# Both FF pairs run alone with block-product down projections, and the sample's attention moves beside the prompt's projections

## The chip, the cores and the metric

One core of a Trainium2 chip runs the whole kernel. The metric is device time in microseconds (us) of one execution, lower is better; of several executions the median is taken. Beside it stands one execution recorded by the hardware profiler, from which all rows below come. Engines: PE (TensorE, with its weight loads as PEld), DVE (VectorE), ACT (ScalarE), POOL (GpSimd), SP (SyncE, which issues nearly all DMAs).

## The reference, cut to what matters

Two independent sequences go through the same two layers: a prompt of 1024 rows and a sample of 512 rows, each 1024 wide. All is float32.

```
def run_trunk(x):                      # x_prompt (1, 1024, 1024), x_sample (1, 512, 1024)
    x = x + fourier_mixer(x, ...)                       # layer 0: FFT over rows and groups, then @ w
    x = x + swiglu_ffn(x, ...)
    x = x + attention_mixer(x, ...)                     # layer 1
    x = x + swiglu_ffn(x, ...)

def attention_mixer(x, g, w_qkv, q_gain, k_gain, w_o, cos, sin):
    q, k, v = split(rms_norm(x, g) @ w_qkv)             # 8 query heads, 2 key/value heads of 128
    q = apply_rope(rms_norm(q, q_gain), cos, sin)       # norm per head; k in the same way
    p = softmax(q @ k.T * 128 ** -0.5)                  # each query head with its group's k
    return (p @ v) @ w_o

def swiglu_ffn(x, g, w_gate, w_up, w_down):             # D_FF = 2816
    h = rms_norm(x, g)
    return (silu(h @ w_gate) * (h @ w_up)) @ w_down
```

## The kernel before, in words

**Tiles.** Activations lie transposed: 128 channels on the partitions, 512 rows along the free dimension. So the sample is one block (block 0) of 8 chunks of 128x512, the prompt two (blocks 1 and 2). D_FF is NF = 22 chunks of 128. Each float32 operand is split into a rounded high part and a remainder (`split`: ACT casts, POOL or DVE subtracts), and each product is three matmuls (`mm3`: high x high, high x low, low x high), the lines L255, L256 and L257 of the profile. Weights are loaded by SP (L289) and split by ACT and POOL (L293, L294).

**Stages.** Mixing of the sample; FF of the sample's layer 0 (`ffn(0, 0)`) beside mixing of the prompt (`aux_0`); "pair 0", the FF of both prompt blocks together in layer 0 (`ffn_pair`), beside the sample's layer-1 chain (`aux_1`: `qkv(0)`, `attend((0,), ...)`, `out_projection(0)`, `prepare(0, 1)`, the norm ahead of its FF); the sample's last FF (`ffn(1, 0)`) beside the prompt's layer 1 up to its FF (`aux_2`: `qkv(2)`, `qkv(1)`, `attend((1, 2), ...)`, two output projections, `moving`); then "pair 1" alone, to the end.

**A pair.** `moving` makes seven operands (`OPERANDS`: B11, B21, T2, T1, B22, T3, N4) from the normed two blocks and stores them in DRAM (`mov`). Gate and up are computed as seven block products instead of eight: for each couple of FF chunks f0, f0+1, `step` runs `times` for each operand, eight products each, with the weights' sums made by POOL (`operands`, `stationary`). The operands come through a ring of eight buffers, unless `places` gives one a place of its own, where it stays after its first load. `times` calls `some` after each product, which adds a credit, and with a whole credit takes one item from the list `pend`: products of the down projection, which run one couple of chunks behind.

**Two ways down.** With `wide` False (pair 0), `down` adds for each block and each of 8 output chunks the products of the two FF chunks, and DVE adds their sum to the accumulator at L1019. With `wide` True (pair 1), `product` runs seven block products (`CHAINS`) of four output chunks each, on operands that `operands_down` and `values_of` make, and DVE adds each at L1107. `wide` also pins some POOL operations in program order (`keep`), takes another order of turns, and loads a21 and a22 earlier.

**Attention.** `qkv` makes twelve heads for one block: eight q, two k, two v. Each is a projection (`project`, 24 matmuls), a square for the head's norm, rotary products on ACT and DVE, four small matmuls that sum the squares (L1341), and a store to DRAM (`dqk`, `dv`). For k, `rstd_cols` and `in_rows` follow (four diagonal tiles by ACT, a matmul with ones each: L322, L323). `attend` takes for each head and each 128 query rows three steps: `scores` (products, a maximum on DVE at L1398, its scaling at L1399, the exponential on ACT at L1402, reciprocal and scaling at L1403 and L1404), `turned` (transposes at L1416, and their splits), and for each two of them `values`. The steps of neighbours overlap: scores of the next come before the transposes of the last.

**The order.** `weave(main, main_cost, aux, aux_cost, lead)` draws from two generators in turn: each yields an estimate of its work in us, and the one that is behind, as a share of its cost, goes next; `lead` steps of the main one go first. Main draws from the buffer rings ending in F, aux from those in X (`cur`; `BUFS` has their depths: w weights, raw loads, t temporaries, g and c banks of PSUM). The framework then orders each engine's instructions by its own model of their times, in which program order is the priority; a buffer ring that is full makes the next tile wait. While pair 0 runs, the X rings are small (`narrow`, `thin()`). SP's DMAs are in one queue.

Of the kernel before, what the change touches and what calls it, by code (L numbers as in the profile page):

```python
# [17 lines left out]
P = 128  # L18
# [107 lines left out]
def trunk_kernel(ctx: ExitStack, tc: tile.TileContext, t: dict):  # L126
# [18 lines left out]
    for name, kw in (("sbH", {}), ("sbF", {}), ("sbX", {}), ("psF", PS), ("psX", PS)):  # L145
# [46 lines left out]
    narrow = [False]  # L192

    def thin():

        return narrow[0] and cur[0] == "X"

# [6 lines left out]
    def side():  # L204

        return bankg() if cur[0] == "F" else bank() if thin() else bank2()[:, 0]
# [110 lines left out]
    def in_rows(y, temp=None, ps=None):  # L317

        r = bank() if ps is None else ps
        for j in range(4):  # L320
            dg = (temp or tmp)(P)
            act.activation(dg, ident, AF.Copy, scale=y[:, j : j + 1])  # L322
            pe.matmul(r[:, j * P : (j + 1) * P], ones, dg, start=True, stop=True)  # L323
        return r
# [36 lines left out]
    def normed(b, gain, got, ab, held=None):  # L361
# [4 lines left out]
        if thin():  # L366
            r, seen = tl("r", [TB], F32, "ssX"), r
            act.copy(r, seen)
        h = h_tile(ab)
        yield 1.0  # L370
        for dp in range(NC // 2):
            for dc, ps in zip((2 * dp, 2 * dp + 1), (None, None) if thin() else sides()):
# [5 lines left out]
                ps = x if ps is None else ps  # L378
# [553 lines left out]
    def ffn_pair(layer, blocks, ring, places, wide, outs):  # L932
# [37 lines left out]
        keep = pinned if wide else lambda ins: ins  # L970
# [23 lines left out]
        wds, coming = {}, {}  # L994

        def load_down(fc):
            coming[fc] = raw_tile(D)
            sp.dma_start(coming[fc], t["down"][layer, fc])

        def fetch_down(fc):  # L1000
            wds[fc] = w_tile(2, NC, P)
            flat = wds[fc].rearrange("p h c n -> p h (c n)")
            split(flat[:, 0], flat[:, 1], coming.pop(fc), eng=pool)

        def down(b, parts, dc, begins, ends):

            box, acc = [], accs[b][dc]

            def half(k):
                n, fc = parts[k]  # L1010
                m, wd = slots[n], wds[fc]
                open_[n] -= 1
                if k == 0:
                    box.append(bank())
                    if begins:
                        sp.dma_start(acc, xres[b][:, dc, :])
                mm3(box[0], wd[:, 0, dc], wd[:, 1, dc], m[:, 0], m[:, 1], k == 0, k + 1 == len(parts))
                if k + 1 == len(parts):
                    dve.tensor_tensor(acc, box[0], acc, op=ALU.add)  # L1019
                    if ends:  # L1020
                        new_residual(b, dc, acc, None if outs is None else outs[b][:, dc, :], room=spare, later=sums_of(b, dc))

            return [lambda k=k: half(k) for k in range(len(parts))]

        mids = {b: [] for b in blocks}
        two = [tl("mid", [2, TB], F32R, "mid") for _ in range(2)]
        if wide:
            spots = two + [tl("mid", [2, TB], F32R, "m2", raws) for _ in range(4)] + [ring[:, 7]]
            spots = dict(zip(("M11", "T1", "T2", "T3", "M22", "M21", "N4"), spots))
            f11, f12 = (tl("f", [TB], F32, "f2", raws) for _ in range(2))  # L1030
        else:
            slots = [two[0], two[1], tl("mid", [2, TB], F32R, "m2", raws), ring[:, 7]]
        open_ = [0] * 4
        where = {(0, 0): (0, 1), (0, 1): (1, 0), (1, 1): (2, 2), (1, 0): (3, 3)}

        def downs(b, f0):

            parts, mids[b] = mids[b], []
            lists = [down(b, parts, dc, f0 == 0, f0 + 2 == NF) for dc in range(NC)]
            for k in range(len(parts)):  # L1040
                pend.extend([lists[0][k], lists[1][k]])
            for v in lists[2:]:
                pend.extend(v)
# [46 lines left out]
        def product(k, d, f0):  # L1090
# [50 lines left out]
        def before_down(f0):  # L1141

            if not wide:
                downs(blocks[1], f0)
            elif f0 == 0:
                load_acc(blocks[0], 0)
# [22 lines left out]
        turn = [0]  # L1169

        TURNS = (tuple((i, j) for j in range(4) for i in range(2)), ((0, 0), (0, 1), (1, 0), (0, 2), (0, 3), (1, 1), (1, 2), (1, 3)))

        def times(w, name, f0, hook, at):

            turn[0] += 1
            if turn[0] % 2 == 0 and not wide:
                banks = [bankg(), bankg()]
            else:
                g2 = tl("a", [2, TB], F32, "gT", gt)
                banks = [g2[:, 0], g2[:, 1]]  # L1180
            at_hand, xs = name in places and f0 > 0, {}
            for n, (i, j) in enumerate(TURNS[wide]):
# [14 lines left out]
        def hidden(up, s, fc, k):  # L1197
            dve.tensor_tensor(up, up, s, op=ALU.mult)
            n = where[fc % 2, k][fc // 2 % 2]
            assert not open_[n], (fc, k)  # L1200
            open_[n] = NC
            m = slots[n]
            split(m[:, 0], m[:, 1], up)
            mids[blocks[k]].append((n, fc))

# [7 lines left out]
        def operands():  # L1213

            a11, a12 = quarter(0, 0), quarter(0, 1)
            for f0 in range(0, NF, 2):
                yield stationary(a11)
                if not (wide and f0):
                    a21, a22 = quarter(f0 + 1, 0), quarter(f0 + 1, 1)
                s1 = tl("raw", [2, TB], F32, "rT", raws) if wide else raw_tile(2, TB)  # L1220
# [12 lines left out]
                if wide and f0 + 2 < NF:  # L1233
# [14 lines left out]
        for f0 in range(0, NF, 2):  # L1248
            f1 = f0 + 1
            gates = {}  # L1250

            def finish(k, ps, s):

                if wide:
                    values_of(k, ps, gates[k], s)
                else:
                    hidden(ps, s, *((f0, 0), (f0, 1), (f1, 1), (f1, 0))[k])
# [16 lines left out]
            for i, ps in (yield from step("T1", lambda: load_rows_down(f0) if wide else load_down(f0), 0)):  # L1274
                plus(V[i], ps, U[i])
            for i, ps in (yield from step("B22", lambda: prepare_down(f0) if wide else (fetch_down(f0), load_down(f1)), 0)):
# [5 lines left out]
            for i, ps in (yield from step("T3", lambda: next(preps[-1]) if wide else fetch_down(f1), 0)):  # L1282
# [6 lines left out]
            for i, ps in (yield from step("N4", lambda: before_down(f0), 0 if wide else 1)):  # L1289
# [5 lines left out]
            if wide:  # L1295
                pend.extend(lambda k=k, d=d, f0=f0: product(k, d, f0) for k in range(7) for d in range(4))
            else:
                downs(blocks[0], f0)
        while pend:
            pend.pop(0)()  # L1300
        close_pool("gT")
# [3 lines left out]
    def qkv(b, held=None):  # L1305
# [6 lines left out]
        ssq = cols.tile([P, 4, NH], F32, tag="ssq", name=nm("ssq"))  # L1312
        for j in range(NH + 2 * NKV):
# [403 lines left out]
```

## Time and profile before

| | |
|---|---|
| median of 3 executions | 2982.39 us (2978.16 to 2984.53) |
| profiled execution | 2986.82 us, span 2984.9 us from the first to the last instruction |
| granted TensorE clock, mean | 0.987 |
| PE busy | 2881.0 us, 97%, 13788 matmuls |
| DVE, ACT, POOL busy | 1606.1, 1281.3 and 1421.0 us |
| DMA | 559.73 MB, 188 GB/s in the mean |

A group's row reads: line, engine, operation, tiles written <- read, shapes, xcount | busy us, mean ns of one | idle time of the engine just ahead of these, and what ended most of it. A row by stage gives the stretch and its width, then busy us and (xcount) of PE, PEld, DVE, ACT and POOL, the granted clock, the DMA engines' share and GB/s. A row of waits says who waited for whom: us in total, times, longest. A row of one line's instructions gives their shortest, median and longest duration in ns, and the first and last start. Matmuls overlap their neighbours, so the mean duration of one is longer than the spacing of two.

### The profile page before, as it was taken

The numbers are of one execution on the slowest core, as the hardware profiler recorded it, in microseconds if no ns is written. First come the engines' busy times: TensorE is split into PE (matmuls) and PEld (weight loads), VectorE is DVE, ScalarE is ACT, GpSimd is POOL, SyncE is SP. The second block draws the span as 40 slices with busy tenths as digits, with TensorE's granted clock in tenths as the row PEclk, the third lists the DMA queues.
The fourth block names the chain that finished last, engine by engine and source line by source line (L and its number), as shares of the span: only waits on it lengthen the run. The fifth ranks groups of instructions, "written<-read, shape, count | busy, mean of one in ns | idle before, by whom it ended". The sixth has DMA issues, their size and how long they took to land. (4 is left out here: it accounts for less than half of the span.)

```text
span 2984.9 us, 37275 instructions
## 1 busy us (share of the span) xinstructions
PE 2881.0 (97%) x13788; PEld 2378.8 (80%) x13788; DVE 1606.1 (54%) x2822; ACT 1281.3 (43%) x2032; POOL 1421.0 (48%) x833
## 2 busy tenths in 40 slices
PE   7999999999999999999999999999998999999999
PEld 6878877878888787877788778788876778888887
DVE  6665553453436554346434365555426366666666
ACT  5543242333325564223444367777534333333332
POOL 4344365545434445434433311212345666776774
PEclk8999999999999999999999999999999999999999
DMA  7335484887767667776533311211457966556553
GB/s 225 142 120 174 150 302 144 289 271 253 245 234 242 222 225 255 270 257 225 190 112 111 104 53 40 78 40 64 129 185 261 332 233 231 192 184 219 200 173 126
DMA packets 201333, 559.73 MB, mean 188 GB/s; under 512 B 21984, under 2 KB 32224, under 8 KB 200256
## 3 DMA queue, kind: packets, MB, share of 16 engines
q1 hardware_dynamic: 200224, 552.57, 54.4%
q0 software_dynamic: 640, 3.74, 0.4%
q8 instruction: 108, 1.77, 0.2%
q10 hardware_dynamic: 288, 1.05, 0.1%
q14 instruction: 73, 0.60, 0.1%
HBM read 489.12 MB, written 68.16 MB: 187 GB/s over the span
## 5 line engine op out<-in xcount | busy, mean ns | idle before, releaser
L294 POOL TENSOR_TENSOR w<-raw,w 128x1024 fp32r<-128x1024 f32 x200 | 479.2, 2404 | 816.6 <-ACT w L293 793.9
L249 POOL TENSOR_TENSOR w<-raw,w 128x512 fp32r<-128x512 f32 (+1 forms) x420 | 577.2, 1396 | 553.1 <-ACT w L248 549.2
L248 ACT CAST w<-raw 128x512 fp32r<-128x512 f32 (+1 forms) x420 | 261.3, 655 | 455.8 <-PE a L257 127.8
L293 ACT CAST w<-raw 128x1024 fp32r<-128x1024 f32 x200 | 208.7, 1049 | 286.3 <-PE g L257 78.8
L255 PE MATMUL c<-mid,w 128*128 128x512 f32 x748 | 295.1, 395 | 14.6 <-DVE acc L1019 7.0
L257 PE MATMUL c<-mid,w 128*128 128x512 f32 x748 | 292.6, 391 | 2.3 <-POOL w L294 2.3
L256 PE MATMUL c<-mid,w 128*128 128x512 f32 x748 | 292.8, 391 | 2.0 <-DVE mid L249 2.0
L255 PE MATMUL g<-h,w 128*128 128x512 f32 x704 | 281.1, 399 | 9.7 <-ACT w L293 7.7
L257 PE MATMUL g<-h,w 128*128 128x512 f32 x704 | 279.4, 397 | 3.3 <-POOL w L294 3.3
L256 PE MATMUL g<-h,w 128*128 128x512 f32 x704 | 279.2, 397 | 0.0
L255 PE MATMUL a<-ring,w 128*128 128x512 f32 x664 | 262.4, 395 | 5.7 <-DVE ring L249 4.5
L257 PE MATMUL a<-ring,w 128*128 128x512 f32 x664 | 259.4, 391 | 0.0
L256 PE MATMUL a<-ring,w 128*128 128x512 f32 x664 | 259.3, 390 | 0.0
L1019 DVE TENSOR_TENSOR acc<-c,acc 128x512 f32<-128x512 f32 x176 | 120.8, 688 | 148.9 <-PE c L257 143.5
L256 PE MATMUL c<-h,w 128*128 128x512 f32 x480 | 190.1, 396 | 4.2 <-POOL h L249 2.8
L255 PE MATMUL c<-h,w 128*128 128x512 f32 x480 | 190.6, 397 | 2.4 <-ACT h L251 1.7
L257 PE MATMUL c<-h,w 128*128 128x512 f32 x480 | 188.5, 393 | 0.0
L792 DVE TENSOR_TENSOR acc<-c,acc 128x512 f32<-128x512 f32 x176 | 120.5, 687 | 122.1 <-PE c L257 121.2
L255 PEld LDWEIGHTS c<-mid,w 128*128 128x128 f32 x748 | 140.5, 188 | 51.5 <-DVE acc L1019 10.6
L257 PEld LDWEIGHTS c<-mid,w 128*128 128x128 f32 x748 | 140.5, 188 | 32.5 <-POOL w L294 3.6
L256 PEld LDWEIGHTS c<-mid,w 128*128 128x128 f32 x748 | 140.7, 188 | 31.8 <-DVE mid L249 3.6
L255 PEld LDWEIGHTS g<-h,w 128*128 128x128 f32 x704 | 134.1, 191 | 36.9 <-ACT w L293 8.5
(393 smaller groups left out, 6564.7 us busy)
## 6 DMA issues: line engine op xcount, KB each, us to landing
ring<-mov_B SPq DMA_DIRECT2D x248, 512.0 KB, 5.5
ring<-mov_T SPq DMA_DIRECT2D x176, 512.0 KB, 5.1
raw<-in_gate_dram SPq DMA_DIRECT2D x44, 512.0 KB, 3.5
raw<-in_up_dram SPq DMA_DIRECT2D x44, 512.0 KB, 3.6
raw<-in_down_dram SPq DMA_DIRECT2D x88, 256.0 KB, 3.1
raw<-in_gate_dram SPq DMA_DIRECT2D x88, 256.0 KB, 5.0
raw<-in_up_dram SPq DMA_DIRECT2D x88, 256.0 KB, 5.3
raw<-in_down_dram SPq DMA_DIRECT2D x44, 512.0 KB, 4.7
```

Of the source, the lines that this page charges most:

```text
L248: keep(act.copy(hi, src))
L249: keep(eng.tensor_tensor(lo, src, hi.bitcast(F32), op=ALU.subtract))
L255: pe.matmul(out, lh, rh, start=first, stop=False, **kw)
L256: pe.matmul(out, lh, rl, start=False, stop=False, **kw)
L257: pe.matmul(out, ll, rh, start=False, stop=last, **kw)
L293: pinned(act.copy(flat[:, 0], raw)) if early else act.copy(flat[:, 0], raw)
L294: pool.tensor_tensor(flat[:, 1], raw, flat[:, 0].bitcast(F32), op=ALU.subtract)
L792: dve.tensor_tensor(acc[dc], box[0], acc[dc], op=ALU.add)
L1019: dve.tensor_tensor(acc, box[0], acc, op=ALU.add)
```

## The change

Pair 0 takes the way down of pair 1, and the plain way and `wide` go; the pair's places (T1, T3, N4 stay in SBUF) hold for both. Nothing is woven into either pair. At the end of the pair its last 28 products stand behind a `yield None`; for pair 0, `main_1` begins between them, at half of its pace. `main_1` is the sample's layer-1 chain with `ffn(1, 0)` behind it, now the main stream beside `aux_2`. The small X rings (`narrow`) go. The sample's attention uses F rings: scores in the g banks, p in the t ring, the transposed p in the w ring. In `qkv`, what follows a head's rotary products (sums, key norm, transposes of v) is kept in a list `owed` and runs after the next head's products (`settle`); the store of q no longer waits for the sums. `in_rows` has a ring of its own for its diagonal tiles, two deep.

```diff
+        "mT": 1, "WT": 1, "rT": 6, "gT": 2, "m2": 4, "f2": 2, "s1": 1, "mv": 3,
...
     def in_rows(y, temp=None, ps=None):
-            dg = (temp or tmp)(P)
+            dg = temp(P) if temp else cols.tile([P, P], F32, tag="dg", name=nm("dg"), bufs=2)
...
     def ffn_pair(layer, blocks, ring, places, outs):
-        keep = pinned if wide else lambda ins: ins
+        keep = pinned
...
-            if fresh:
+            if fresh and f0 + 2 < NF:
                 chain[d] = bank() if d % 2 else bankg()
+            elif fresh and d % 2 == 0:
+                g2 = tl("a", [2, TB], F32, "gT", gt)
+                chain[d], chain[d + 1] = g2[:, 0], g2[:, 1]
...
-            credit[0] = min(credit[0] + (0.8 if wide else 0.85), 1.7)
+            credit[0] = min(credit[0] + 0.8, 1.7)
...
-            if wide:
-                pend.extend(lambda k=k, d=d, f0=f0: product(k, d, f0) for k in range(7) for d in range(4))
-            else:
-                downs(blocks[0], f0)
+            pend.extend(lambda k=k, d=d, f0=f0: product(k, d, f0) for k in range(7) for d in range(4))
+        yield None
         while pend:
             pend.pop(0)()
+            yield 1.4
...
     def qkv(b, held=None):
-        rope = tl("rope", [2, TB], F32, "pX", ap)
+        rope = tl("rope", [2, TB], F32, "pX", ap) if cur[0] == "X" else tl("rope", [2, TB], F32, "mid")
...
+        owed = []
+        def sums(j, sq):
+            c = bank()
+            for i in range(4):
+                pe.matmul(c[:, i : i + 1], sq[:, i * P : (i + 1) * P], ones[:, 0:1], start=True, stop=True)
+            dve.tensor_copy(ssq[:, :, j], c[:, 0:4])
+        def key_sums(j, sq, a):
+            y = cols.tile([P, 4], F32, tag="yk", name=nm("yk"))
+            rstd_cols(y, sq, HD)
+            owed.append(lambda: key_rows(j, y, a))
+        def key_rows(j, y, a):
+            r = in_rows(y)
+            dve.tensor_tensor(a, a, r, op=ALU.mult)
+            sp.dma_start(dqk[b][j], a)
...
+        def settle():
+            now, owed[:] = owed[:], []
+            for v in reversed(now):
+                v()
...
+            if cur[0] == "F" and j == NH:
+                keys = tl("keys", [NKV, TB], F32, "mid")
+            sq, a, sw = tmp(), keys[:, j - NH] if cur[0] == "F" and j >= NH else tmp(), side()
...
-            yield 5.5
+            settle()
             if j < NH:
-                c = bank()
...
+                sp.dma_start(dqk[b][j], a)
+                owed.append(lambda j=j, sq=sq: sums(j, sq))
             else:
-                y = cols.tile([P, 4], F32, tag="yk", name=nm("yk"))
-                rstd_cols(y, sq, HD)
-                yield 2.0
...
+                owed.append(lambda j=j, sq=sq, a=a: key_sums(j, sq, a))
+            yield 6.0 if j < NH else 8.0
...
     def attend(blocks, straight, slot):
-                    sc = bank().unsqueeze(1) if thin() else bank2()
+                    sc = bankg().unsqueeze(1) if nb == 1 else bank2()
-                    p = tmp(T) if thin() else tl("p", [T], F32, "pX", ap)
+                    p = tmp(T) if nb == 1 else tl("p", [T], F32, "pX", ap)
...
-    def aux_1():
+    def main_1():
         yield from qkv(0)
         yield from attend((0,), 0, "A")
         yield from out_projection(0, "A")
         yield from prepare(0, 1)
+        yield from ffn(1, 0, h_next, t["y"][0])
     def aux_2():
+        for b in (2, 1):
+            settled(b)
+            yield 2.0
...
-    weave(last["pair"], 0.9 * PAIR_US, aux_1(), CHAIN_US, 24)
...
-    weave(ffn(1, 0, h_next, t["y"][0]), 0.85 * FFN_US, aux_2(), PROMPT_US, 9)
-    weave(last["pair"], 1.0)
+    through(last["pair"])              # up to the yield None
+    one, due = main_1(), 0.0
+    for v in last["pair"]:
+        due += 0.5 * v
+        while due > 0.0:
+            due -= next(one)
...
+    weave(one, CHAIN_US + 0.85 * FFN_US, aux_2(), PROMPT_US, 0)
+    through(last["pair"])
+    for _ in last["pair"]:
+        pass
```

FFN_US, PAIR_US, CHAIN_US and PROMPT_US are 352, 678, 223 and 630.

More of the change, by code (lines that the diff above doesn't have):

```diff
@@ L204, in side @@
     def side():
-        return bankg() if cur[0] == "F" else bank() if thin() else bank2()[:, 0]
+        return bankg() if cur[0] == "F" else bank2()[:, 0]
     def sides():
@@ L930, in moving, with ffn_pair @@
         close_pool("mv")
-    def ffn_pair(layer, blocks, ring, places, wide, outs):
+    def ffn_pair(layer, blocks, ring, places, outs):
         src = (t["gate"], t["up"])
@@ L992, in ffn_pair @@
         credit = [0.0]
[L994 to L1023, printed above, removed]
@@ L1034, in ffn_pair @@
[L1034 to L1043, printed above, removed]
+        two = [tl("mid", [2, TB], F32R, "mid") for _ in range(2)]
+        spots = two + [tl("mid", [2, TB], F32R, "m2", raws) for _ in range(4)] + [ring[:, 7]]
@@ L1167, in stationary @@
             return w
-        turn = [0]
-        TURNS = (tuple((i, j) for j in range(4) for i in range(2)), ((0, 0), (0, 1), (1, 0), (0, 2), (0, 3), (1, 1), (1, 2), (1, 3)))
+        TURNS = ((0, 0), (0, 1), (1, 0), (0, 2), (0, 3), (1, 1), (1, 2), (1, 3))
         def times(w, name, f0, hook, at):
[L1175 to L1180, printed above, removed]
+            g2 = tl("a", [2, TB], F32, "gT", gt)
+            banks = [g2[:, 0], g2[:, 1]]
             at_hand, xs = name in places and f0 > 0, {}
-            for n, (i, j) in enumerate(TURNS[wide]):
+            for n, (i, j) in enumerate(TURNS):
                 if i == 0:
@@ L1195, in times @@
             return list(enumerate(banks))
[L1197 to L1204, printed above, removed]
         def silu(s, x):
@@ L1248, in ffn_pair @@
         for f0 in range(0, NF, 2):
-            f1 = f0 + 1
             gates = {}
             def finish(k, ps, s):
[L1254 to L1257, printed above, removed]
+                values_of(k, ps, gates[k], s)
             def gated(k, s, x):
@@ L1273, in ffn_pair @@
                 plus(U[i], ps, U[i])
-            for i, ps in (yield from step("T1", lambda: load_rows_down(f0) if wide else load_down(f0), 0)):
+            for i, ps in (yield from step("T1", lambda: load_rows_down(f0), 0)):
                 plus(V[i], ps, U[i])
-            for i, ps in (yield from step("B22", lambda: prepare_down(f0) if wide else (fetch_down(f0), load_down(f1)), 0)):
+            for i, ps in (yield from step("B22", lambda: prepare_down(f0), 0)):
                 plus(ps, ps, V[i])
@@ L1281, in ffn_pair @@
                     finish(1, ps, s)
-            for i, ps in (yield from step("T3", lambda: next(preps[-1]) if wide else fetch_down(f1), 0)):
+            for i, ps in (yield from step("T3", lambda: next(preps[-1]), 0)):
                 plus(U[i], ps, U[i])
@@ L1288, in ffn_pair @@
                     finish(2, ps, s)
-            for i, ps in (yield from step("N4", lambda: before_down(f0), 0 if wide else 1)):
+            for i, ps in (yield from step("N4", None if f0 else lambda: load_acc(blocks[0], 0), 0)):
                 plus(ps, ps, U[i])
@@ L1543, in aux_0, with paired @@
         close_pool("mp")
-        yield from paired(0, {}, False, None)
-    def paired(layer, places, wide, outs):
+        yield from paired(0, None)
+    def paired(layer, outs):
         ring = h_slot("ring", F32R, "B")[:, 0 : 16 * TB].rearrange("p (s h n) -> p s h n", s=8, h=2)
@@ L1551, in paired @@
         close_pool("psX")
-        last["pair"] = ffn_pair(layer, (1, 2), ring, places, wide, outs)
+        last["pair"] = ffn_pair(layer, (1, 2), ring, {"T1": here, "T3": late, "N4": late}, outs)
         cur[0] = "F"
@@ L1592, in aux_2, with through @@
         close_pool("ap")
-        yield from paired(1, {"T1": here, "T3": late, "N4": late}, True, t["y"])
-    late_ = []
-    def here():
-        if "mT" not in pools:
-            open_pool("mT", **RIGHT)
-        return tl("op", [4, 2, TB], F32R, "mT", pools["mT"])
-    def late():
-        if not late_:
-            two = h_slot("late", F32R, "A")[:, 0 : 16 * TB].rearrange("p (k c h n) -> p k c h n", k=2, c=4, h=2)
-            late_.extend([two[:, 0], two[:, 1]])
-        return late_.pop(0)
-    narrow[0] = True
-    BUFS.update({"wX": 3, "rawX": 1, "ssX": 1, "pX": 1, "mT": 1, "gT": 1})
+        yield from paired(1, t["y"])
+    def through(pair):
+        for v in pair:
+            if v is None:
+                return
+    through(last["pair"])
[4 more added lines that the diff above has]
+            due -= next(one)
+    close_pool("mT")
+    late_.clear()
     open_pool("sbX", **RIGHT)
```

77 lines of the change are left out of this document (29 added, 48 removed), and 1 row of the table BUFS.

## The prediction

> **What bounds the kernel now.** I read the page first, for the engine totals and the groups; then busy time by stage, for which stage loses time; then the waits of the matmul engine in the lossy stages; then single groups, for the chains behind those waits.
>
> ```profile
> span 2984.9 us, 37275 instructions
> PE 2881.0 (97%) x13788; PEld 2378.8 (80%) x13788; DVE 1606.1 (54%) x2822; ACT 1281.3 (43%) x2032; POOL 1421.0 (48%) x833
> L1019 DVE TENSOR_TENSOR acc<-c,acc 128x512 f32<-128x512 f32 x176 | 120.8, 688 | 148.9 <-PE c L257 143.5
> L1107 DVE TENSOR_TENSOR acc<-g,acc 128x512 f32<-128x512 f32 x154 | 105.7, 686 | 53.9 <-PE g L257 53.7
> L1107 DVE TENSOR_TENSOR acc<-c,acc 128x512 f32<-128x512 f32 x154 | 105.7, 686 | 45.8 <-PE c L257 44.9
> ```
>
> TensorE has work in 97% of the span and nothing else passes 54%, so time goes only with fewer matmuls or with less idle time between them. The last three rows show the two ways down: pair 0 closes 176 plain sums (two blocks, 8 output chunks, 11 pairs of FF chunks), pair 1 adds 2 x 154 = 308 block products (7 x 4 x 11).
>
> The stages, cut at the first and last rows of their own lines: first moves of pair 0 with ffn 0's end, sample's qkv, its attention, its output projection, end of pair 0, start of ffn 1 with prompt's qkv, the rest of that, prompt's attention, its output projections, change to pair 1, pair 1, its end.
>
> ```profile
> core 0: us, PE busy (x) PEld busy (x) DVE busy (x) ACT busy (x) POOL busy (x), PEclk, DMA share, GB/s
> 534.00:622.00 88.00, 84.92 (x365) 68.26 (x364) 53.84 (x79) 31.89 (x57) 46.83 (x28) 0.96 0.87 306
> 622.00:890.00 268.00, 266.24 (x1218) 220.56 (x1217) 106.25 (x187) 81.81 (x132) 123.94 (x74) 1.00 0.73 251
> 890.00:1150.00 260.00, 252.31 (x1242) 208.92 (x1241) 150.47 (x277) 152.18 (x258) 116.09 (x75) 0.99 0.70 232
> 1150.00:1340.00 190.00, 187.28 (x829) 153.96 (x828) 74.94 (x122) 53.15 (x88) 89.77 (x53) 0.99 0.75 263
> 1340.00:1425.00 85.00, 78.88 (x342) 63.08 (x341) 60.94 (x79) 31.06 (x49) 35.33 (x19) 1.00 0.66 229
> 1425.00:1465.00 40.00, 37.12 (x159) 30.11 (x158) 20.40 (x35) 17.29 (x25) 22.69 (x10) 0.91 0.64 214
> 1465.00:1700.00 235.00, 233.53 (x1124) 191.53 (x1123) 92.82 (x207) 93.68 (x139) 88.63 (x37) 1.00 0.35 110
> 1700.00:2130.00 430.00, 409.84 (x2364) 345.71 (x2362) 252.11 (x472) 304.46 (x430) 97.89 (x42) 0.99 0.18 58
> 2130.00:2300.00 170.00, 161.66 (x724) 131.19 (x725) 62.72 (x113) 59.77 (x91) 84.73 (x46) 0.99 0.65 220
> 2300.00:2400.00 100.00, 83.38 (x336) 66.11 (x335) 41.06 (x62) 32.37 (x56) 66.85 (x43) 0.91 0.90 330
> 2400.00:2950.00 550.00, 550.00 (x2418) 451.99 (x2417) 357.33 (x545) 195.60 (x350) 391.44 (x276) 1.00 0.58 196
> 2950.00:2985.00 35.00, 29.55 (x124) 22.33 (x122) 28.57 (x46) 7.25 (x13) 8.63 (x7) 0.99 0.32 120
> ```
>
> Two readings. Pair 1 alone has no idle time at all in 550 us, with VectorE at 65% and GpSimd at 71%; its 2418 matmuls, all 512 wide, give 550.00/2418 = 0.2275 us each. (The mean duration of one such matmul in the groups is 0.39 us, because neighbours overlap; the spacing is what a removed one gives back.) And I count as loss of a stage its idle time plus the time that the granted clock took, (1 - PEclk) x width: 6.6, 1.8, 10.3, 4.6 and 6.1 for the five stages from 534 to 1425, then 6.5, 1.5, 24.5, 10.0 and 25.6 up to 2400. Together 97.5 us.
>
> **The change, part by part.**
>
> *Pair 0 down as block products.* The plain way is 2 blocks x 8 chunks x 22 FF chunks = 352 products, the new one 7 x 4 x 11 = 308; each is three matmuls. So 44 x 3 = 132 matmuls go, at 0.2275 us: **-30.0 us**. In exchange come 308 - 176 = 132 more accumulations on DVE (x 0.686 = 91 us) and the operand sums and splits on POOL, ACT and DVE. They cost nothing while pair 1's row of 2400 to 2950 holds, since it is this very load with no idle time. Its DMA share of 0.58 is also under the 0.70 to 0.75 of pair 0 now: three of seven operands stay in SBUF and SP issues their loads once. The pinned order and the wider buffers are in pair 1's row too. Bounds: 0 to 7 (the loss now in pair 0's first 88 us, in which the sample's chain begins); taken 2.
>
> *The chain leaves pair 0.* Its matmuls go to the next stage, so their sum is unchanged; what changes is what covers its waits. The five losses, 29.4 us in all, end here and come back below as far as the chain carries them along.
>
> *Pair 0's end and the restart.* Today it costs 6.1 + 6.5 = 12.6.
>
> ```profile
> PE c L255 <- DVE acc L1019: 6.1, 4, 2.6
> PE c L323 <- ACT t L322: 2.9, 1, 2.9
> ```
>
> DVE ends the waits at the end, then the diagonal matmuls of the next norm wait for ACT. In the new tail stand 28 accumulations, 14 sums of squares and the 16 DVE operations of the sample's norm, 58 x 0.69 = 40 us of DVE, over 28 x 3 + 2 x 24 = 132 matmuls = 30 us of PE (the tail pulls some 20 us of main_1, which is the norm and two heads). So up to 10 us more can show, unless heads 2 and on fill it. rope and the block sums also sit in buffers of the pair (mid, tF). Bounds 6 (the DVE wait gone or hidden) to 23; taken 12.6, since the head projections behind it are ready work, as ffn 1 is now.
>
> *Sample's qkv and attention beside the prompt's qkv.* Pieces carried along: 1.8 + 10.3 from the chain, 1.5 from 1465 to 1700. New: block 1's norm must wait for block 2's heads to leave the h buffer, and the dense ffn no longer covers it but a chain full of waits does; I add 5, an estimate from the 2.9 above and three DVE and ACT steps of 0.7. Taken 18.6, bounds 9 (norm covered, waits of attention thinned by wider buffers) to 64 (last rival).
>
> *Head sums one head later.* The four small matmuls of the head sums now come after the next head's projection.
>
> ```profile
> L1341 PEld LDWEIGHTS c<-ones,t 128*128 128x128 f32 x192 | 23.9, 191 | 4.0 <-ACT t L1331 3.4
> ```
>
> Over all 36 heads PE lost 3.4 us on the squares, and the price is a square held one head longer, in rings of three and four buffers; key heads hold a second tile, for which the sample's stream gets its own. Between -3 and +3; taken 0. The diagonals of in_rows move to a two-buffer ring: each waits for the matmul of the one before last; inside the same bounds.
>
> *Prompt's attention beside more.* Now the output projection of the sample and ffn 1 run beside it, at paces of 522 against 630 where it was 299 against 630. Its 258 us of yields now stand beside 214 us of main work instead of 122, and those yields are worth their time in matmuls (ffn: 1584 x 0.2275 = 360 against 358 of yields). Per step (64) that is 3.3 us of filler instead of 1.9.
>
> ```profile
> PE a L255 <- ACT p L1402: 11.8, 10, 1.8
> PE a L257 <- POOL w L249: 3.5, 2, 2.2
> ```
>
> The scores wait for the exponential to free their one double bank; a wait of at most 1.8 us shrinks with 1.4 us more filler per step. Loss now 24.5, and 4.6 of the output projection: 29.1. If it falls as filler grows, 29.1 x 122/214 = 17; taken 17, bounds 10 to 29.
>
> *Sample's second norm* (prepare) was covered by pair 0; now only prompt attention covers it. No row shows it there: 0 (attention covers) to 10 (twice the 1340 to 1425 DVE wait with a clock drop); taken 5, nearest the 2.9 of L322.
>
> *To pair 1.* 35.6 us from 2130 to 2400, mostly this:
>
> ```profile
> PE g L255 <- ACT w L293: 7.7, 1, 7.7
> PE a L255 <- DVE ring L249: 4.5, 1, 4.5
> ```
>
> When aux_2 ends, about 34 us of ffn yields are left where 44 were, so slightly less cover; 32 to 45, taken 35.6. Before 534 and after 2400 nothing is touched.
>
> Sum: 2 + 12.6 + 18.6 + 17 + 5 + 35.6 = 90.8 against 97.5, so -6.7, with -30.0 makes -36.7. The profiled execution took 2986.8 (span 2984.9 and 1.9 around it); it becomes 2950. It lies 4.4 above the median of 2982.4, so the median becomes **2946**.
>
> **The rivals.**
>
> *A. The idle time thins further.* All lower bounds hold: 0 + 6 + 9 + 10 + 0 + 32 = 57, so -30 - 40 = -70: 2912. For it: the row with no idle time. Against: the change to pair 1 is no thinner.
>
> *B. Each restart costs.* The tail at 23, block 1's norm and prepare at 10 each instead of 5: 20 more, 2966. For it: both restarts in the table stand at PEclk 0.91. Against: there are ready projections at both.
>
> *C. Slower: the sample's attention lies bare.* A step of a head goes through these in turn:
>
> ```profile
> L1398 DVE TENSOR_REDUCE col<-c 128x1 f32<-128x512 f32 x32 | 22.0, 689 | 17.7 <-PE c L257 17.6
> L1399 DVE SCALAR_TENSOR_TENSOR col<-col,nrqc x96: 207/219/2337, 900.6 to 2125.4; 128x1 f32<-128x1 f32 x96
> L1402 ACT ACTIVATE t<-c,col,rqc 128x512 f32<-128x512 f32 x32 | 24.9, 779 | 35.3 <-DVE col L1399 35.0
> L1403 DVE RECIPROCAL col<-col 128x1 f32<-128x1 f32 x96 | 15.3, 160 | 52.1 <-ACT p L1402 38.0 <-ACT t L1402 14.1
> L1404 ACT ACTIVATE t<-t,col 128x512 f32<-128x512 f32 x32 | 22.7, 723 | 5.4 <-DVE col L1403 5.4
> L248 ACT CAST w<-c 128x512 fp32r<-128x512 f32 x32 | 18.7, 583 | 9.9 <-PE c L1416 9.6
> L249 DVE TENSOR_TENSOR w<-c,w 128x512 fp32r<-128x512 f32 x32 | 22.0, 689 | 16.5 <-ACT w L248 16.3
> ```
>
> That is 2.57 us from scores to transposes and 1.27 us to the values: 3.84 x 32 steps = 123 us if nothing covers. Beside pair 0 it cost 10.3, with a yield of 2.2 worth one step. A head of the prompt yields 6.0, which at 522 to 630 is worth 5.0 us, six or seven steps in a row. If half lies bare, 61 in place of 13.6 counted: 2946 + 48 = 2994, slower; it decides from about 50 us bare, 40%. Against it: the engine doesn't run in the order of the yields, for even the three matmuls of a product are parted by those of another stream:
>
> ```profile
> 534.55 0.50 PE L255 MATMUL c<-mid,w 128*128 128x512 f32 x1
> 534.89 0.39 PE L256 MATMUL a<-ring,w 128*128 128x512 f32 x1
> 535.12 0.40 PE L257 MATMUL a<-ring,w 128*128 128x512 f32 x1
> ```
>
> so projections with weights at hand can fill a burst. Idle time also lowers the clock here:
>
> ```profile
> 1704.00:1712.00 8.00, 5.16 (x23) 3.60 (x21) 4.11 (x15) 4.19 (x5) 6.52 (x3) 0.97 0.48 172
> 1712.00:1714.50 2.50, 2.50 (x7) 1.96 (x6) 2.46 (x3) 1.68 (x2) 2.50 (x2) 0.50 0.61 193
> ```
>
> After 2.84 us of idle time within 8, the clock stood at half. [...]
>
> **How the numbers follow.** Forecast (2934 to 2958): 0.45. A (2912 to 2934, or below): 0.20. B (2958 to 2976): 0.16. C: 0.19, of which 0.06 within 6 us of no change and 0.13 slower. 0.2%, 6 us, is about what a measurement of this kernel can tell. So faster 0.81, same 0.06, slower 0.13. The range runs from A's bottom, 2912, to B's top, 2976, and leaves out C's 0.19.
>
> **What would show it.** 13656 matmuls; 616 accumulations at the block products' line and none at the plain one; about 600 us with no idle time, ending near 1175; pair 1 alone from about 2285; prompt's attention at under 17 us of loss. If the count is right and the time isn't, the loss between 1175 and 2300 says which term failed: over 64 us beside the sample's attention is C, gaps at the restarts are B. If pair 0 alone shows idle time, the first term's cover was wrong.

## The result, and the profile after

The changed kernel takes 2964.08 us in the median (2962.74 to 2968.29, 4 runs) against 2983.46 for the kernel before; the ratio is 0.9942 (0.9926 to 0.9957). It is faster by some 17 to 19 us; 36 were forecast. The time lies inside the range given, but the gain is about half of what was forecast. The profiled execution took 2965.4.

The page of the changed kernel, its span, engine totals and the groups that answer to those shown of before (the line of the block products is now L1054; the plain line is gone):

```profile
span 2963.6 us, 37198 instructions
PE 2855.9 (96%) x13656; PEld 2350.0 (79%) x13656; DVE 1713.3 (58%) x3031; ACT 1304.9 (44%) x2131; POOL 1517.6 (51%) x932
L1054 DVE TENSOR_TENSOR acc<-g,acc 128x512 f32<-128x512 f32 x280 | 192.5, 687 | 106.9 <-PE g L251 106.6
L1054 DVE TENSOR_TENSOR acc<-c,acc 128x512 f32<-128x512 f32 x280 | 192.4, 687 | 93.7 <-PE c L251 92.1
```

132 matmuls are gone, as counted. 560 accumulations stand here; the other 56 write from tiles called `a`, of which more below.

To see where the time went, I cut each execution at the same matmuls: the first 2600 (ahead of pair 0, where the two kernels issue the same ones, in nearly the same order), the last 2000 (pair 1's), and what lies between. Busy time by these three stretches, of before and then of after, in the same columns as the stage table of the prediction:

```profile
0.00:542.60 542.60, 514.86 (x2600) 431.88 (x2601) 308.68 (x612) 223.57 (x356) 254.89 (x131) 0.97 0.53 177
542.60:2522.60 1980.00, 1909.17 (x9189) 1573.34 (x9189) 992.22 (x1743) 897.88 (x1391) 851.40 (x480) 0.99 0.56 191
2522.60:2985.00 462.40, 456.95 (x2001) 373.56 (x1999) 305.16 (x468) 159.86 (x286) 314.67 (x222) 1.00 0.55 187
```

```profile
0.00:547.70 547.70, 514.32 (x2600) 431.10 (x2601) 308.06 (x613) 219.66 (x353) 246.98 (x128) 0.98 0.53 178
547.70:2491.00 1943.30, 1878.38 (x9058) 1545.05 (x9057) 1096.87 (x1951) 925.32 (x1493) 955.06 (x582) 0.99 0.47 161
2491.00:2964.00 473.00, 463.24 (x2001) 373.81 (x1999) 308.37 (x468) 159.92 (x286) 315.51 (x222) 0.99 0.53 182
```

The middle, where the whole sum of the prediction stands, became 36.7 us shorter: the very sum that was forecast. But the stretch ahead of pair 0 became 5.1 longer and pair 1's 2000 matmuls about 10 longer, and both had been priced at nothing ("Before 534 and after 2400 nothing is touched"). -36.7 + 5.1 + 10.3 = -21.3, the difference of the spans (the last rows run past the spans' ends, 2984.9 and 2963.6, by 0.1 and 0.4). These are single executions: in after_beside, another one of the changed kernel, the middle took 1946.5. And 2600 matmuls from the start are not an exact mark: the first 1000 took between 215 and 224 us in all the kernels, for reasons that come at the end of the experiments. The 1602 behind them are steadier, below.

The stages of the changed kernel, by its own marks: pair 0 alone, its end, qkv of sample and prompt, the sample's attention, its output projection and second norm with the start of the prompt's attention, the rest of that, output projections, change to pair 1:

```profile
534.00:1155.00 621.00, 618.77 (x2721) 508.02 (x2720) 395.36 (x614) 225.22 (x405) 444.26 (x312) 1.00 0.61 209
1155.00:1215.00 60.00, 53.06 (x229) 38.51 (x228) 55.77 (x84) 33.72 (x54) 21.21 (x12) 1.00 0.54 182
1215.00:1345.00 130.00, 128.50 (x639) 105.97 (x639) 62.01 (x160) 62.74 (x95) 48.96 (x21) 1.00 0.42 135
1345.00:1510.00 165.00, 151.23 (x845) 122.75 (x844) 107.04 (x251) 118.09 (x223) 42.62 (x23) 1.00 0.24 76
1510.00:1640.00 130.00, 112.88 (x592) 93.95 (x591) 70.32 (x151) 75.33 (x114) 35.62 (x15) 0.95 0.37 125
1640.00:2005.00 365.00, 351.60 (x2011) 296.57 (x2010) 200.91 (x366) 255.53 (x358) 92.62 (x39) 1.00 0.20 66
2005.00:2190.00 185.00, 185.00 (x839) 153.38 (x837) 48.52 (x90) 51.91 (x73) 82.13 (x39) 1.00 0.47 154
2190.00:2310.00 120.00, 107.81 (x450) 86.19 (x450) 55.30 (x83) 42.13 (x64) 68.23 (x39) 0.95 0.77 273
```

By the prediction's own count (idle time and granted clock) these lose 2.2, 6.9, 1.5, 13.8, 23.6, 13.4, 0 and 18.2 us, 79.6 together for 97.5 before. That is 17.9 less, where the middle shows some 7 beside the count of matmuls: about 10 us stand in no idle row. The count is coarse (the clock is rounded, and a short wait hides under matmuls that overlap, 0.39 us long at a spacing of 0.2275), so it serves to compare terms and not to add up to the time.

### The profile page after: what moved, and what is told of

The parts are those of the page before. It is cut to its first block, busy times and chain, and to the rows that moved or that the text cites. A ratio compares the mean times of both kernels' runs of the same rounds, so it can differ in the third digit from the quotient of the medians.

```text
span 2963.6 us, 37198 instructions
## 1 busy us (share of the span) xinstructions
PE 2855.9 (96%) x13656; PEld 2350.0 (79%) x13656; DVE 1713.3 (58%) x3031; ACT 1304.9 (44%) x2131; POOL 1517.6 (51%) x932
## 5 line engine op out<-in xcount | busy, mean ns | idle before, releaser
L243 POOL TENSOR_TENSOR w<-raw,w 128x512 fp32r<-128x512 f32 (+1 forms) x464 | 608.3, 1331 | 451.2 <-ACT w L242 445.0
L242 ACT CAST w<-raw 128x512 fp32r<-128x512 f32 (+1 forms) x464 | 279.6, 632 | 538.3 <-PE a L251 173.2
L249 PE MATMUL a<-ring,w 128*128 128x512 f32 x712 | 279.5, 392 | 0.1
L251 PE MATMUL a<-ring,w 128*128 128x512 f32 x712 | 277.5, 390 | 0.0
L250 PE MATMUL a<-ring,w 128*128 128x512 f32 x712 | 277.3, 389 | 0.0
L1054 DVE TENSOR_TENSOR acc<-g,acc 128x512 f32<-128x512 f32 x280 | 192.5, 687 | 106.9 <-PE g L251 106.6
L1054 DVE TENSOR_TENSOR acc<-c,acc 128x512 f32<-128x512 f32 x280 | 192.4, 687 | 93.7 <-PE c L251 92.1
L249 PE MATMUL c<-mid,w 128*128 128x512 f32 x592 | 232.4, 393 | 13.3 <-ACT mid L242 7.6
L250 PE MATMUL c<-mid,w 128*128 128x512 f32 x592 | 232.6, 393 | 1.2 <-DVE mid L243 1.1
L251 PE MATMUL c<-mid,w 128*128 128x512 f32 x592 | 232.5, 393 | 1.3 <-POOL w L288 1.3
L782 DVE TENSOR_TENSOR acc<-c,acc 128x512 f32<-128x512 f32 x176 | 120.9, 688 | 129.2 <-PE c L251 126.5
L249 PEld LDWEIGHTS g<-h,w 128*128 128x128 f32 x704 | 133.0, 189 | 37.1 <-ACT w L287 3.8
L249 PEld LDWEIGHTS a<-ring,w 128*128 128x128 f32 x712 | 133.8, 188 | 33.8 <-DVE mid L243 4.4
L251 PEld LDWEIGHTS g<-h,w 128*128 128x128 f32 x704 | 132.9, 189 | 30.0 <-POOL w L288 3.3
```

The lines of the kernel that those rows point to most:

```text
L242: keep(act.copy(hi, src))
L243: keep(eng.tensor_tensor(lo, src, hi.bitcast(F32), op=ALU.subtract))
L249: pe.matmul(out, lh, rh, start=first, stop=False, **kw)
L250: pe.matmul(out, lh, rl, start=False, stop=False, **kw)
L251: pe.matmul(out, ll, rh, start=False, stop=last, **kw)
L782: dve.tensor_tensor(acc[dc], box[0], acc[dc], op=ALU.add)
```

## The experiments

The ratio behind each median is to the kernel before, on the same chip.

**The end of pair 1.** The last 120 matmuls took 29 us before and 40 now, and PE's waits among them are for DVE and ACT, none for a DMA. DVE alternates with PE there. Its timeline in after:

```profile
2943.87 1.42 DVE L1054 TENSOR_TENSOR acc<-a,acc 128x512 f32<-128x512 f32 x2 [0.33 <-PE a L251]
2945.62 1.41 DVE L1054 TENSOR_TENSOR acc<-a,acc 128x512 f32<-128x512 f32 x2 [0.33 <-PE a L251]
```

PE's weight loads in the same stretch:

```profile
2944.61 0.19 PEld L249 LDWEIGHTS a<-mid,w 128*128 128x128 f32 x1 [0.49 <-DVE acc L1054]
2945.34 0.19 PEld L249 LDWEIGHTS a<-mid,w 128*128 128x128 f32 x1 [0.19 <-DVE acc L1054]
2946.36 0.19 PEld L249 LDWEIGHTS a<-mid,w 128*128 128x128 f32 x1 [0.50 <-DVE acc L1054]
```

Two products are issued every 1.75 us (2944.61 to 2946.36), where six matmuls at 0.2275 are 1.37. Each couple of output chunks shares a double bank (`a`, from the gate/up ring). The first of the two adds that begin at 2945.62 ends at half of 1.41 us, 2946.33, and the next product begins at 2946.36: each product waits for the add of the last but one. It looks as if a double bank let in one product or one add at a time; which half a product writes, the rows don't show. e1_last gives pair 1 its four single banks again:

```diff
-            if fresh and f0 + 2 < NF:
+            if fresh and (f0 + 2 < NF or layer):
```

> Pair 1's last seven block products (28 products) go back to four single banks (two c, two g), as before the change; pair 0 keeps the two double banks of the gate/up ring. Theory T (double banks couple neighbours: PE's next product into a double bank waits for both additions, 3.5 us per four products where 2.7 would do): the last 120 matmuls take 29 us again instead of 40, median about 2953, ratio to the kernel before about 0.990. Rival (pair 1's end is long because the products wait for the last gate values, whatever the banks): no change, 2964.

Measured: 2961.35 us, 0.9941 (0.9923 to 0.9959). In its trace the end is nearly as before the change (462.4):

```profile
550.00:2494.10 1944.10, 1878.50 (x9058) 1545.16 (x9057) 1096.51 (x1951) 926.89 (x1493) 954.92 (x582) 0.99 0.48 161
2494.10:2958.00 463.90, 457.01 (x2001) 373.53 (x1999) 304.78 (x468) 160.17 (x286) 315.24 (x222) 1.00 0.54 186
```

463.9 for 473.0, with the middle unchanged. The spacing explains some 5 us of it (14 times 1.75 - 1.37, an estimate), and a stretch of 6.8 us at half clock, which is in the last section and not in e1_last, 3.4. But 2953 was expected: the median gained only 3, and the first 2600 matmuls took 550. That is taken up again at the end.

e1_single makes the gate/up ring four single banks, for both pairs:

```diff
-            g2 = tl("a", [2, TB], F32, "gT", gt)
-            banks = [g2[:, 0], g2[:, 1]]
+            banks = [tl("a", [TB], F32, "gT", gt) for _ in range(2)]
...
-            elif fresh and d % 2 == 0:
-                g2 = tl("a", [2, TB], F32, "gT", gt)
-                chain[d], chain[d + 1] = g2[:, 0], g2[:, 1]
+            elif fresh:
+                chain[d] = tl("a", [TB], F32, "gT", gt)
```

> The gate/up ring of PSUM as four single banks in place of two double ones, in both pairs; the last products of both pairs take single banks from it. Theory T: both ends gain; pair 1's end as in e1_last or 2 to 3 us worse (those banks must first be freed by the last gate and up products), pair 0's end some 3 to 5 us, so 2950 to 2956. If tracking by tile has nothing to do with it: 2964, as the changed kernel.

2959.28 us, 0.993 (0.9915 to 0.9944). The same four banks, tracked one by one, bring the last 120 matmuls to 28.5 us, so the coupling is the cause and not the ring. Pair 0's end, where 3 to 5 us were expected, gained nothing by it: the sums of squares then wait 3.6 us for the last accumulation.

**The stretch ahead of pair 0.** e2_front takes the diagonal tiles from the t rings until pair 0 begins:

```diff
-            dg = temp(P) if temp else cols.tile([P, P], F32, tag="dg", name=nm("dg"), bufs=2)
+            dg = (temp or tmp)(P) if not own_dg else cols.tile([P, P], F32, tag="dg", name=nm("dg"), bufs=2)
...
+    own_dg.append(1)
     through(last["pair"])
```

> The diagonal tiles of in_rows come from the t rings again, until pair 0 begins; the own two-deep ring serves only behind it. Nothing else ahead of pair 0 differs from the kernel before. Theory: the 5 us that the stretch ahead of pair 0 lost (first 2600 matmuls 547.7 us against 542.6) came from this ring, through another order on ACT; they take 543 again, median about 2959. Rival (the order ahead of pair 0 is changed by what pair 0 now loads: its places and six raw buffers): 547 and 2964.

2959.04 us, 0.9927 (0.9913 to 0.994). The same 1602 matmuls, 1000 to 2600, of before:

```profile
222.40:542.60 320.20, 315.24 (x1602) 266.71 (x1602) 157.45 (x319) 107.91 (x159) 162.03 (x78) 1.00 0.56 187
```

Of after:

```profile
222.30:547.70 325.40, 316.53 (x1602) 267.66 (x1601) 157.79 (x320) 104.17 (x156) 153.59 (x75) 0.99 0.56 190
```

Of e2_front:

```profile
217.30:536.90 319.60, 314.60 (x1602) 266.73 (x1602) 157.92 (x320) 105.40 (x157) 153.87 (x75) 1.00 0.57 193
```

So the diagonal tiles are worth 5 to 6 us. That e2_front meets the time of before is chance all the same, as the pieces of all 20 traces show (us, shortest and longest):

| matmuls | code of before (4) | own ring (6) | t rings (10) |
|---|---|---|---|
| 1800 to 2200 | 91.3 to 93.5 | 97.3 to 100.4 | 91.3 to 94.5 |
| 2200 to 2560 | 84.9 to 87.7 | 81.6 | 81.6 |
| 2560 to 2600 | 9.3 to 9.4 | 11.7 to 12.0, e3_plain 9.3 | 11.7 to 13.4 |

The own ring costs about 6 us in the first row. The rest of the change gains 3 or more in the second, whatever the ring, and loses 2.4 in the third, where pair 0's first products come in another order. For after that is 6.0 - 3.3 + 2.5 = 5.2.

What the tiles do is not done where they stand: the framework put ACT's casts in another order, and one waits for a transfer with others behind it. ACT's longest waits (who waited <- for whom: us in all, times, longest) of after, 380 to 450:

```profile
ACT w L287 <- DMA raw<-in_down_dram: 18.4, 3, 11.5
```

Of e2_front, 370 to 445:

```profile
ACT w L287 <- DMA raw<-in_down_dram: 4.0, 1, 4.0
```

In after PE then waits 3.1 and 2.9 us for casts queued behind (`ring`, `mid`); in e2_front for neither longer than 0.4.

**The count alone.** e3_plain is the changed kernel with pair 0's plain way down put back (the old `ffn_pair`, with `wide` for pair 1 alone, and the new `yield None` and places).

> The changed kernel with pair 0's plain way down put back (176 sums, 352 products instead of 308), all else as changed: pair 0 alone, its places, the new order. 13788 matmuls. Theory: the 132 matmuls are worth their spacing, 30 us, and the rest of the change is worth about +9 alone: 2994, slower than the kernel before by 0.3 to 0.4%. Rival (mean duration of the rows, 0.39 us each): 3016. Rival (the block products cost back in DVE and POOL what they save): 2970 to 2980.

2982.01 us, 1.0002 (0.9992 to 1.0013). Its pair 1 keeps single banks to the end, so it is to be held against e1_last:

```profile
540.60:2514.00 1973.40, 1906.41 (x9190) 1574.93 (x9189) 971.66 (x1743) 872.64 (x1372) 851.88 (x483) 0.99 0.47 159
2514.00:2977.00 463.00, 456.99 (x2001) 373.54 (x1999) 305.18 (x468) 160.19 (x286) 315.01 (x222) 1.00 0.55 187
```

1973.4 - 1944.1 = 29.3 us for 132 matmuls, 0.222 each. In the middle the spacing was the right price and the mean duration of a row, 0.39, was not, and the added DVE and POOL work cost next to nothing. The medians, on the same chip, are only 20.7 apart. In the traces e1_last loses 9.4 us on its first 2600 matmuls: 2.4 of it in the last 40 (the table), and some 7 by stretches at half clock that e3_plain's trace lacks. (From 60 to 115 us the granted clock was 0.91 in e1_last and 1.00 in e3_plain.) So the price rests on the middle of two traces, with some 3 us of scatter. Without the count, the rest of the change is worth nothing in the median (1.0002). My expectation of 2994 had forgotten that this kernel's end is not lengthened: 10 less is 2984.

**Both terms mended, and four things on that base.** c1_both is e1_single with e2_front.

> The changed kernel with both repairs: four single banks in the gate/up ring, and in_rows on the t rings ahead of pair 0. Theory (the two terms priced at nothing, 11 and 5 us, add up): matmuls 1000 to 2600 take 320 us, the last 120 take 28.5, median about 2950, ratio to the kernel before about 0.990, some 15 under the changed kernel. If the order the framework makes shifts the loss elsewhere: 2955 to 2960.

2946.01 us, 0.9881 (0.9866 to 0.9896): the forecast time, but with more mended than its working had seen. The middle is 1946.2, the end 461.2. That it is the forecast of 2946 is chance.

e4_sums_at_once puts the head sums back behind their head (and the key norms and the transposes of v behind theirs):

```diff
-            settle()
+            yield 5.5
             if j < NH:
+                sums(j, sq)
                 sp.dma_start(dqk[b][j], a)
-                owed.append(lambda j=j, sq=sq: sums(j, sq))
```

> c1_both with the head sums at once, as before the change (sums, key norm and transposes of v directly behind their head's rotary products; stores of q wait for the sums). Prediction's term: within 3 us of c1_both. Rival (the deferred sums are what lets the prompt's heads fill the sample's attention): 10 or more slower, with waits of the small sum matmuls on the squares between 1190 and 1510.

2963.9 us, 0.9934 (0.9921 to 0.9947): 18 slower than c1_both in the median, 13.6 in the middle stretch of the traces. Cut at the same matmuls, some 13 of it come up beside the sample's attention, where 215 us hold fewer of them. c1_both, from 1288:

```profile
1288.00:1503.00 215.00, 201.23 (x1085) 165.09 (x1084) 129.06 (x321) 137.43 (x255) 53.51 (x28) 0.98 0.25 79
```

e4_sums_at_once, from 1295:

```profile
1295.00:1510.00 215.00, 191.86 (x990) 154.81 (x988) 120.53 (x302) 131.22 (x246) 48.66 (x26) 0.96 0.24 78
```

PE's waits of e4_sums_at_once in that stretch, who waited <- for whom: us, times, longest:

```profile
PE c L1364 <- ACT t L1352: 5.2, 4, 2.0
PE c L249 <- DVE ssq L1238: 4.1, 6, 2.1
PE c L317 <- ACT dg L316: 3.8, 1, 3.8
```

The middle row is the copy of the sums, which holds the bank that the next product needs; the matmuls of the sums themselves waited only 1.1 us for the squares. In c1_both that row is absent. How much of the 13.6 is these waits, and how much another alignment of the streams, this run doesn't separate.

e6_main_fast and e6_main_slow shift the main stream against the prompt's (1.15 and 0.85; 0.9 and 0.7 in two further runs):

```diff
-    weave(one, CHAIN_US + 0.85 * FFN_US, aux_2(), PROMPT_US, 0)
+    weave(one, 1.15 * (CHAIN_US + 0.85 * FFN_US), aux_2(), PROMPT_US, 0)
```

> c1_both with the cost of the main stream 15% up, so that it is drawn ahead of the prompt's: its second norm and its FF begin earlier against the prompt's attention, and less FF is left for the change to pair 1. Theory (cover decides both losses): the stretch from the sample's output projection to the first gate product loses 5 to 10 us less than the changed kernel's 24, the change to pair 1 loses 10 to 20 more than its 18: 2955 to 2965. Rival (these losses are latency whatever stands beside): both stay, 2950.

> c1_both with the cost of the main stream 15% down, so that it is drawn later: more FF is left beside the change to pair 1, and the sample's second norm falls later into the prompt's attention. Theory: the change to pair 1 loses up to 8 us less than 18, the second norm as much as now (about 15) or more: 2945 to 2952. Rival as above: 2950.

e6_main_fast: 2962.87 us, 0.9932 (0.992 to 0.9944). e6_main_slow: 2941.14, 0.9858 (0.9845 to 0.987). With the FF drawn early, it was used up when the change to pair 1 came, and one wait for a moving operand stood bare:

```profile
PE a L249 <- DVE x L917: 25.3, 1, 25.3
```

So cover decides there, in one direction. Further steps:

> c1_both with the cost of the main stream 10% down, between 2946 (0%) and 2941 (15%). If loss follows the cover smoothly: 2940 to 2947. If alignment decides: anywhere from 2930 to 2965, with the difference in one or two places.

> c1_both with the cost of the main stream 30% down. If the gain of the 15% step came from FF kept for the change to pair 1, a further step gains little there (that loss is near its floor of 5) and leaves FF alone at the end: 2938 to 2948. If the order in general is best balanced near 15%, it is slower than 2941.

c90_main_slow: 2941.52, 0.9868 (0.9853 to 0.9883). e8_main_slower: 2966.8, 0.9948 (0.9931 to 0.9964), its loss now at the prompt's attention, which lost its FF (1690 to 1760: 56.35 us of PE busy in 70, clock 0.83). The optimum is flat between 10 and 15% and falls off on both sides.

e5_fine draws each projection in four parts; e9_slow_fine does so at the pace of e6_main_slow:

```diff
-            project(w, h, ps)
+            for dc in range(NC):
+                part(w, h, ps, dc)
+                if dc in (1, 3, 5):
+                    yield 1.5
```

> c1_both with each qkv projection drawn in four parts (1.5 us of yields each), so that the sample's attention steps no longer come six or seven in a row. Theory of the last rival of the prediction (bursts lay the attention bare): the stretch of the sample's attention, 14 us of loss in the changed kernel, falls to about 5 and the median to 2937. Other theory (the framework's order of each engine already evens the bursts out): within 3 us of 2946.

> Both at once: main stream 15% down and the projections in four parts. If the bursts matter: 2932 to 2937. If not: 2941, as with the pace alone.

2949.77 us, 0.9899 (0.9882 to 0.9916), and 2954.43, 0.9911 (0.9896 to 0.9926). Bursts in the text's order are not what costs: evening them out gained nothing, and at the slower pace it cost 13.

**Is it the deferral, or the alignment?** The deferral alone, in the prompt's heads of the kernel before (with a two-deep ring for their diagonal tiles):

> The kernel before with one thing of the change: the prompt's heads settle their sums, key norms and v transposes one head later (the sample's qkv as it was). Theory (the deferral is worth 13 to 18 us only beside a chain of waits; the dense FF already covered it): within 4 us of the kernel before, since its prompt qkv beside the FF lost only 1.5 us from 1465 to 1700. Rival (the deferral is worth as much anywhere): 2965 to 2970.

2955.27 us, 0.9917 (0.99 to 0.9935). My theory, no effect where the FF covers, fell. But the gain isn't at the heads. The change to pair 1, same width, in before:

```profile
2245.00:2400.00 155.00, 134.47 (x555) 106.76 (x554) 73.51 (x112) 53.46 (x89) 97.47 (x62) 0.94 0.85 310
```

In e7:

```profile
2230.00:2385.00 155.00, 148.97 (x633) 119.63 (x633) 78.42 (x117) 58.22 (x96) 105.01 (x66) 0.98 0.90 327
```

78 more matmuls in it, about 18 of the 25 us that the middle became shorter (1954.5), some 600 us behind the heads. Two kernels shift the streams of the kernel before by 6% and nothing else (0.80 or 0.90 x FFN_US for 0.85):

> The kernel before with the cost of its last FF at 0.80 x 352 in place of 0.85: FF is drawn a little later against the prompt. Theory (alignment): the loss between 2250 and 2400, 29 us in the kernel before, moves by 10 or more either way, and the median with it: 2960 to 2995, not 2980. Rival (the deferral itself): loss and median within 4 us of the kernel before.

> The kernel before with the cost of its last FF at 0.90 x 352: FF is drawn a little earlier, less of it left for the change to pair 1. Theory (alignment): the loss at the change to pair 1 moves by 10 or more; 2960 to 3000. Rival: within 4 us of the kernel before.

2972.73 us, 0.9975 (0.9966 to 0.9984), and 2974.93, 0.9981 (0.9971 to 0.9991). In the same 155 us they issue 592 and 586 matmuls, so either shift takes 7 or 8 us off the change to pair 1 (in b90_before_pace 3 of them were lost again earlier). Alignment alone explains some 8 of the 18; whether the rest is the deferral's own or a luckier alignment stays open.

**The two terms in the medians.** Three kernels on one chip:

> The changed kernel itself, as it was, to stand beside the next two on one chip: 2964 as before, ratio to the kernel before 0.994.

> The end of pair 1 alone mended, as in e1_last, on the chip of after_beside. If the end's 11 us reach the time: 9 to 12 under after_beside. If another loss takes their place: within 4 of it.

> The end of pair 1 as in e1_last and the diagonal tiles ahead of pair 0 as in e2_front, and nothing else. If both terms reach the time: 14 to 17 under after_beside, 2948. If not: 2955 to 2960.

2965.97 us, 0.9948 (0.9936 to 0.9961); 2962.07, 0.9937 (0.9925 to 0.995); 2951.34, 0.9897 (0.9883 to 0.991). Both terms together are 14.6 in the medians. The traces of after_beside and c2_end_front differ by 14.7: 8.9 at the end, 3.8 in matmuls 1000 to 2600, 1.4 ahead of these and 0.6 in the middle.

The end alone shows 4 in the medians, where 9 to 12 were expected, and 9 in the traces. The granted clock can account for the rest: its mean over the six executions is 0.9872 for e1_last_beside and 0.9890 for after_beside, and 0.0018 of 2960 us is an estimated 5 us. The traces place such differences in the first 120 us, far ahead of the edit; the engines' order of instructions is the same in both kernels up to matmul 2600. Two executions of one program, after and after_beside, took 112 and 108 us for the first 500 matmuls, with a granted clock of 0.83 and 0.89 in the first 60 us. (The own ring adds 2 us there: matmuls 400 to 450 take 11.0 us or more with it and 9 without.) Whether e1_last's lower clock is scatter, six executions of each don't settle.

## Why the prediction was wrong, point by point

- **Count of matmuls and price of each: right.** 13656, and 29.3 us measured for 30.0 in the middle stretch.
- **Pair 0 alone: right.** 2.2 us of loss, 2 taken, ending near 1211 with the last accumulation (1175 was named).
- **"Before 534 and after 2400 nothing is touched": the step that failed.** After 2400 the diff touches the last couple of FF chunks of both pairs, since `f0 + 2 < NF` holds no layer. The prediction counts DVE's work at pair 0's end and names the double banks at neither. Size 10 us, of which single banks give back 9 to 12. Ahead of 534 it touches `in_rows`, which I had put into the deferral's bounds of 3 as a wait of its own, and which acted through ACT's order: 6 us, and 5 with what else moved there. With both mended the median is 2946.0 (c1_both) or 2951 (c2_end_front). My sign of what failed, the loss between 1175 and 2300, looked past both.
- **The middle: sum right by luck, terms not.** The 6.7 us beside the count came out as 6.7 at the price of 30.0, within the 3 us by which two executions differ. The end of pair 0 and the sample's attention stayed within their bounds (6.9 for 12.6; 1.5 + 13.8 for 18.6). The output projection, second norm and prompt's attention lost 37.0 for 22: from 1510 to 1640 only the attention stood beside the second norm, with 6.8 us of waits for the exponential and 4.0 for a split. The change to pair 1 lost 18.2 for 35.6. These two errors, +15 and -17, cancelled. With the others the counted sum is 79.6 for 90.8, a gain that the time does not show.
- **Head sums one head later, between -3 and +3, taken 0: mis-sized.** Taking it back costs 14 to 18 us (e4_sums_at_once), alignment included. The row that I priced it by, 3.4 us of waits for the squares, showed one of its waits, in a stage where the FF covered them.
- **To pair 1, 32 to 45, taken 35.6: mis-sized.** e7, b80 and b90 show that this loss is no constant of the kernel before: 29 us counted by spacing there, and 7 to 18 less after small shifts far ahead of it.
- **Rivals.** A did not come: the change to pair 1 fell even below its lower bound, but the prompt's attention rose. C, the bare attention, did not happen (15.3 us of loss, over 64 was its sign), and e5_fine shows that the order of the text was no threat. B's gap at the second norm is there (from 1510 to 1640), paid for elsewhere.

The best kernel run here is e6_main_slow: both terms mended and the main stream 15% down, 2941.14 us, 0.9858 (0.9845 to 0.987); c90_main_slow is the same within its interval.

## What to carry to other kernels

Follow a changed condition to every place where it holds, a helper's new buffers as well, before a stretch is called untouched. Where a framework orders the engines' queues, small edits move single losses far away: a shift of 6% by 7 or 8 us, a deferral by 18. A loss read off one trace is not a constant to carry over, and two such shifts of the old kernel, timed, show how wide the error of a forecast has to be. Cut both traces at the same matmul and compare the stretches, since idle time alone hides short waits under overlapping rows (here of 0.39 us, 0.2275 apart).

## What the runs showed of the hardware

The clock fell to half at the end of pair 1 after waits of which none was longer than 1.2 us. After, the stretch just ahead and the stretch at half clock:

```profile
2919.20:2935.20 16.00, 12.12 (x49) 8.44 (x47) 12.44 (x19) 6.75 (x13) 7.96 (x7) 1.00 0.00 0
2935.20:2942.00 6.80, 5.92 (x15) 4.07 (x14) 3.36 (x5) 0.55 (x1) 0.00 (x0) 0.50 0.00 0
```

PE's waits in the first of them:

```profile
PE a L249 <- DVE acc L1054: 2.6, 3, 1.0
PE a L249 <- ACT f L1076: 1.2, 1, 1.2
```

3.9 us of idle time in 16, in small pieces, were followed by 6.8 us at half clock, in which 15 matmuls were issued (at 0.2275 us it would be 30). In the traces of before and after, such falls go with how the idle time falls into intervals of 3.41 us. The last two ahead of this one:

```profile
2928.40:2931.80 3.40, 2.60 (x10) 1.20 (x8) 3.01 (x5) 1.67 (x3) 3.23 (x3) 1.00 0.00 0
2931.80:2935.20 3.40, 1.57 (x7) 0.97 (x6) 2.82 (x5) 0.62 (x2) 0.00 (x0) 1.00 0.00 0
```

Behind the first 60 us and up to the last matmul, the clock fell 11 times in the trace of before and 9 times in that of after. It stood at half for 3.41 us each time, or for two or three times that (6.83, 10.24), and within a trace all these stretches begin on one grid of 3.413 us. Of the grid's 1679 intervals at full clock in the two traces, all 13 in which PE was busy for under 0.40 of the time were followed by half clock, 7 of the 15 between 0.40 and 0.55, and none of 1651 over 0.55. (Busy is what the profile counts, with modelled ends.) Here it was 0.46. So 1.8 us of idle time within one interval came ahead of a fall here, and 3.1 us that fell into two (after, 91.92 to 98.74, busy for 0.50 and 0.58) did not.
